# Two paired projections and a handful of ordering edges in a two-layer hybrid decoder trunk

## The chip, the core and the metric

The kernel runs on one core of a Trainium2 chip. The core has a matrix engine (TensorE, PE in the profile), a vector engine (VectorE, DVE), a scalar engine (ScalarE, ACT), a general engine (GpSimd, POOL) and a queue engine that issues transfers (SyncE, SP). The metric is the device time of one execution in microseconds (us); the median of several runs is compared.

## The reference

Two layers work on x of 256 rows and 1024 columns, in float32. Every layer normalizes the rows, multiplies by one input matrix of 1024 x 3584, runs three kinds of heads on the result, gates each with a SiLU path, multiplies by an output matrix and adds the input back:

```python
hn = rms_norm(x, norm_gain)
proj = jnp.einsum('bsd,de->bse', hn, w_in)
a_q, a_k, a_v, a_g, b_x, b_g, c_q, c_k, c_v, c_g = jnp.split(proj, _in_split_points(), axis=-1)
...
y_a = dilated_attention(qa, ka, va) * jax.nn.silu(a_g)       # 8 heads, rotary q and k
y_b = rg_lru_branch(b_x, ...) * jax.nn.silu(b_g)             # convolution and linear recurrence
y_c = stick_breaking_attention(qc, kc, vc) * jax.nn.silu(c_g)  # 4 heads
return x + jnp.einsum('bse,ed->bsd', jnp.concatenate([y_a, y_b, y_c], -1), w_out)
```

A final normalization follows the second layer. The dilated heads take softmax over three strided windows; the stick-breaking heads take products of sigmoids along the keys.

## The kernel before

**Products with a rest.** Each float32 operand is held as two parts: a rounded part (hi) and the rest that rounding left (lo). A product is hi*hi + hi*lo + lo*hi. For activations the parts are `xh` and `xl`, which lie side by side in one tile `xx`; for weights they are the tiles `whi` and `wlo`. `load_chunk` (lines 101 to 118) fetches a weight chunk of 128 x 2048 in two transfers on the SP queue, into staging tiles `st` of which there are five. ACT then rounds four pieces of 512 (line 115, `rounds`), and DVE subtracts to get the four rests (line 117, `rests`). The chunks are numbered: 3 and 4 are the stick-breaking q and k (CQ, CK), 5 and 6 the first dilated q and k (four heads each), 7 the input of the recurrence (BX), 8 and 9 the second dilated q and k, 10 to 13 the gates (CG, BG, AG), 14 to 17 the output matrix (O). `ask` requests a chunk two ahead of the one in use.

**Two forms of a projection.** `proj_b` makes the 256 outputs of a chunk as two blocks of 128, with the 256 rows of x as the moving columns. A chunk that isn't in `PAIRED[l]` takes the plain form: one PSUM bank for both blocks, and for each block 3 x 8 products of 256 columns (`mm3`, line 225), hi*xh, hi*xl and lo*xh in turn. A paired chunk takes, for each block, a bank of its own, 8 products of 512 columns, which are hi times xh and xl at once (line 344), and 8 of 256 columns, lo*xh (line 341). The bank then holds the main sum in one half and hi*xl in the other, so ACT copies that half out (`low`, line 347) and DVE adds the two (line 349). There are three banks of this kind (pool `pp`), used in turn.

**The dilated q and k.** `rotated` (line 507) calls `proj_b`, and then DVE applies the rotary table: a shuffle, two products with the table, a sum, and in layer 0 a product with the row scales `rb` (lines 519 to 524). In the plain form these read the PSUM bank; in the paired form they read the sums, of which the first lies in a scratch tile of a pool of seven. Between the two blocks of the first q stand the stick-breaking scores (`sb_scores`): 16 products (line 474), eight sigmoids on ACT, and for each of four heads two scans and a product on DVE (lines 485 and 487). Between the two blocks of the second q stand the scores of the first four dilated heads (line 548).

**The order.** The order of PE's instructions is the order of the program. On the other engines a planner orders the instructions, by its own estimate of when each can start and by program order among those that can. `dep(a, b)` adds an ordering edge: a stands behind b on their engine, with no wait of its own. The kernel has many such edges already. An engine takes its instructions strictly in that order.

**The border of the layers.** At the end of layer 0 the output products of row tile 0 (halves 0 and 1) and then of row tile 1 finish. DVE adds each to the residual `xres` (line 796). `normed` takes the squares on ACT (line 207), the scale through Ln and Exp (line 84) and multiplies on DVE (line 265); `turn` transposes the rows on PE (line 273) and splits them into the two parts (lines 217 and 218). Row tile 0 is normalized during the last output products, and row tile 1 (`xn1`) during layer 1's first products with AV (chunks 0 and 1). ACT and DVE prepare layer 1's weight chunks meanwhile.

Of the kernel before, what the change touches and what calls it, by code (L numbers as in the profile page):

```python
# [12 lines left out]
AF = mybir.ActivationFunctionType  # L13
ALU = mybir.AluOpType
# [28 lines left out]

CH_AV, CH_CV, CH_CQ, CH_CK, CH_BX, CH_CG, CH_BG, CH_AG, CH_O = 0, 2, 3, 4, 7, 10, 11, 12, 14
CH_AQ, CH_AK = (5, 8), (6, 9)
PAIRED = ((CH_BX, CH_AQ[1], CH_AK[1], CH_CG, CH_AG, CH_AG + 1), (CH_CQ, CH_CK, CH_AQ[0], CH_AK[0], CH_BX, CH_AQ[1], CH_AK[1], CH_CG, CH_BG, CH_AG, CH_AG + 1))


@with_exitstack
def trunk_kernel(ctx: ExitStack, tc: tile.TileContext, x, first_x, first, wpack, prm_d, gatew, gains, consts, rope, out):  # L50
    nc = tc.nc
    act, dve, pe, gps = nc.scalar, nc.vector, nc.tensor, nc.gpsimd
# [10 lines left out]
    def bank(pool, tag):  # L63
        return pool.tile([P, 512], F32, name=tag, tag=tag)

    def scr(w):
        return wk.tile([P, 512], F32, name="scr", tag="scr", bufs=SCR)[:, 0:w]
# [3 lines left out]
    def dep(inst, on):  # L71
        tc.add_manual_dep(inst.ins, on.ins.name, nosync)
        return inst
# [9 lines left out]
    def tab(*a, **k):  # L83
        i = dep(act.activation(*a, **k), loaded["load"])  # L84
        loaded["users"].append(i)
        return i
# [7 lines left out]
    def x_tile():  # L94
        xx = sb.tile([P, NK, 2, S], F32R, name="xx", tag="xx")
        return xx, xx[:, :, 0, :], xx[:, :, 1, :]
# [3 lines left out]
    split, rounds, rests = {}, {}, {}  # L100
# [29 lines left out]
    def weights(l, c, ahead=AHEAD):  # L130
        ask(l, c, ahead)
        return ready.pop((l, c))
# [16 lines left out]
    for k in range(NK):  # L149
# [10 lines left out]
        w = st[:, S:1024]  # L160
# [27 lines left out]
    xres = cst.tile([P, NT, D], F32, name="xres")  # L188
# [12 lines left out]
    ones = cst.tile([P, P], F32R, name="ones")  # L201
    dve.memset(ones.bitcast(F32), 1.0)

    def rms_stats(t, eng):
        sq = wk.tile([P, 2], F32, name="sq", tag="sq", bufs=2)
        for i in range(2):
            act.activation(scr(512), xres[:, t, i * 512:(i + 1) * 512], AF.Square, accum_out=sq[:, i:i + 1])
        ss = wk.tile([P, 1], F32, name="ss", tag="ss", bufs=2)
        eng.tensor_scalar(ss, sq[:, 0:1], 1.0 / D, EPS, ALU.mult, ALU.add)
        ln = wk.tile([P, 1], F32, name="lnv", tag="lnv", bufs=2)  # L210
        tab(ln, sq[:, 1:2], AF.Ln, bias=ss, scale=1.0 / D)
        rstd = wk.tile([P, 1], F32, name="rstd", tag="rstd", bufs=4)
        tab(rstd, ln, AF.Exp, scale=-0.5)
        return rstd
# [5 lines left out]
    def mm3(ps, lhs, rhs, ks, first, last, skip=False):  # L220
# [3 lines left out]
        for i, (a, b, k) in enumerate(seq):  # L224
            pe.matmul(ps, a(k), b(k), start=first and i == 0, stop=last and i == len(seq) - 1,  # L225
                      skip_group_check=skip)

    last = {}

    def finish(t, n2, ps=None, c0=0, c1=512):  # L230
        if n2 == 0:
# [27 lines left out]
    def normed(t):  # L259
        rstd = rms_stats(t, gps)  # L260
        xns = []
        for half in range(2):
            xn = scr(512)
            cs = slice(half * 512, half * 512 + 512)
            dve.scalar_tensor_tensor(xn, xres[:, t, cs], rstd, gn[:, cs], ALU.mult, ALU.mult)
            xns.append(xn)
        return xns

# [40 lines left out]
    gn = cst.tile([P, D], F32, name="gn", tag="gn")  # L309

    for l in range(L):
# [14 lines left out]
        def proj_b(c, mid=None, to=None, sc=1.0):  # L326
            pair = c in PAIRED[l]
            hi, lo = [a.rearrange("p (k c) -> p k c", c=256) for a in weights(l, c, AHEAD - 1 if mid else AHEAD)]
# [31 lines left out]
        def proj_to(dst, c, mid=None, sc=1.0):  # L360
            if c in PAIRED[l]:
                proj_b(c, mid, [dst[:, b, :] for b in range(2)], sc)
                if l == 0:
                    dve.tensor_mul(dst, dst, rb.rearrange("p (o t) -> p o t", o=1).broadcast_to([P, 2, S]))
            else:
                scaled(dst, proj_b(c, mid), sc)
# [45 lines left out]
        def scaled(dst, ps, sc=1.0):  # L412
            if l == 0:
                a, b = rows(ps)
                last["scaled"] = dve.scalar_tensor_tensor(dst, a, sc, b, ALU.mult, ALU.mult)
            else:
                act.activation(dst, v2(ps), AF.Copy, scale=sc)
# [31 lines left out]
        def head(h):  # L449
            return slice((h % 2) * HD, (h % 2) * HD + HD), h // 2, slice(h * HD, (h + 1) * HD)  # L450
# [13 lines left out]
        zs, sw = {}, {}  # L464
        halves = ((0, slice(0, 128)), (1, slice(128, 384)))

        def sb_scores():
            for p in (0, 2):
                for h in (p, p + 1):
                    zs[h] = bank(at, "s")  # L470
                for t, cs in halves:
                    for h in (p, p + 1):
                        hr, hb, _ = head(h)
                        pe.matmul(zs[h][:, cs], qc[hr, hb, t * P:(t + 1) * P], kc[hr, hb, 0:(t + 1) * P],  # L474
                                  start=t == 0, stop=True, skip_group_check=True)
            table(SIGM, [split[l, CH_AK[0]]])
            for h in range(NHC):
                z = zs[h][:, 0:384]
                bt, om = scr(384), scr(384)
                tab(om, z, AF.Sigmoid, scale=-1.0)  # L480
                tab(bt, z, AF.Sigmoid)
                w = sw[h] = wk.tile([P, 384], F32, name="sw", tag="sw", bufs=4)
                gps.memset(w[:, 127::256], 0.0)
                for lo, n in ((0, 127), (128, 255)):
                    dve.tensor_tensor_scan(w[:, lo:lo + n][:, ::-1], om[:, lo + 1:lo + 1 + n][:, ::-1],  # L485
                                           diag[:, 255 - n:255][:, ::-1], 0.0, ALU.mult, ALU.add)
                dve.tensor_mul(w, bt, w)

        def turned(tiles, h0, gs, to):
            for g in gs:  # L490
# [17 lines left out]
        def rotated(c, tiles, h0, tag, mid=None):  # L508
            dst = tiles[h0] = sb.tile([P, 2, S], F32, name=tag, tag=tag)
            tab_ = rp0 if l == 0 else rp  # L510
            pair = c in PAIRED[l]
            if pair:
                src, high = scr(S), dst[:, 1, :]
                proj_b(c, mid, [src, high])
            else:
                ps = proj_b(c, mid)
                src, high = ps[:, 0:S], ps[:, S:2 * S]
            sh = scr(S)
            dve.stream_shuffle(sh, src, SHUF)
            dve.tensor_mul(dst[:, 0, :], src, tab_[:, 0, :])  # L520
            dve.tensor_mul(sh, sh, tab_[:, 1, :])
            dve.tensor_add(dst[:, 0, :], dst[:, 0, :], sh)
            if l == 0:
                dve.tensor_mul(dst[:, 1, :], high, rb)
# [111 lines left out]

        if l > 0:
            proj_to(qc, CH_CQ, None, 0.125)
        else:
            cq_ps = proj_b(CH_CQ)  # L640
            tables()
# [6 lines left out]
        if l == 0:  # L648
            for i in range(2):
                dve.tensor_mul(rp0[:, i, :], rp[:, i, :], rb)  # L650
        rotated(CH_AQ[0], qT, 0, "q0", sb_scores)
        rotated(CH_AK[0], kT, 0, "k0")
        split_qk(0, ("yl0", "yh0"))
        sw_t, sw_heads = turned_tile()
# [9 lines left out]

        rotated(CH_AQ[1], qT, 4, "q1", second)
        if l == 0:
            for r in rests[l, CH_CG]:
                dep(r, last["min"])
            for r in last["exps"][4:]:
                dep(r, last["low"])  # L670
            for r in (*last["recs"][2:], *rests[l, CH_CG][1:]):
                dep(r, last["sum"])
# [33 lines left out]
        ps = None  # L706
        if CH_AG in PAIRED[l]:
            agf = sb.tile([P, 2, S], F32, name="agf", tag="cg")
# [10 lines left out]
        if l == 0:  # L719
# [16 lines left out]
            for r in (*rests[l, CH_O][4:], *rests[l, CH_O + 1]):  # L736
                dep(r, last["sum", CH_AG, 0])
        if CH_AG + 1 in PAIRED[l]:
            seeded = last["bank"]
# [8 lines left out]
        o_ps = {}  # L748
# [4 lines left out]
        for n2 in range(2):  # L753
            w = weights(l, CH_O + n2)
# [23 lines left out]
        for t in range(NT):  # L778
            if t == 1 and l == 0:
                next_x = x_tile()  # L780
                xn0 = normed(0)
            for n2 in range(2):
                cs = slice(n2 * 512, n2 * 512 + 512)
                if tail and (t, n2) == (1, 1):
                    for ps, c0, c1 in tail:
                        out_mm(ps, ow[n2], t, 1, range(4), False, True, c0, c1, c0 > 0)
                        if c0 == 0:
                            x_t = xres[:, t, 512:512 + LATE]
                            dve.tensor_add(x_t, ps, x_t)
                        finish(t, n2, None if c0 == 0 else ps, c0, c1)  # L790
                    continue
                for ks in ((0, 1), (2, 3)):
                    out_mm(o_ps[t, n2], ow[n2], t, 1, ks, False, ks[0] == 2)
                    if (l, t, n2, ks[0]) == (0, 1, 1, 0):
                        turn(xn0, 0, *next_x[1:])
                dve.tensor_add(xres[:, t, cs], o_ps[t, n2], xres[:, t, cs])
                if l > 0:
                    finish(t, n2)

# [106 lines left out]
```

## Time and profile before

| what | value |
|---|---|
| median of 3 runs | 245.24 us (244.14 to 245.63) |
| the profiled execution | 245.22 us |
| its span, first to last instruction | 243.3 us |
| PE busy | 235.7 us, 97% of the span |
| PE's weight loads busy | 203.3 us, 84% |
| DVE busy | 202.3 us, 83% |
| ACT busy | 176.8 us, 73% |
| granted TensorE clock | 0.995 of full |
| transfers | 43.88 MB, mean 180 GB/s |

The shares are averages over the span. What an engine's busy time is worth depends on whether something waits for it, so the chain of waits and the order of the queues around a stage count for more than the shares. An instruction's start and length are given in microseconds from the start of the span; weight loads (PEld) run beside products (PE). The recorded lengths of neighbours on DVE and ACT overlap a little; the distance from start to start is what an instruction occupies of its queue.

### The profile page before, as it was taken

The numbers are of one execution on the slowest core, as the hardware profiler recorded it, in microseconds if no ns is written. First come the engines' busy times: TensorE is split into PE (matmuls) and PEld (weight loads), VectorE is DVE, ScalarE is ACT, GpSimd is POOL, SyncE is SP. The second block draws the span as 40 slices with busy tenths as digits, with TensorE's granted clock in tenths as the row PEclk, the third lists the DMA queues.
The fourth block names the chain that finished last, engine by engine and source line by source line (L and its number), as shares of the span: only waits on it lengthen the run. The fifth ranks groups of instructions, "written<-read, shape, count | busy, mean of one in ns | idle before, by whom it ended". The sixth has DMA issues, their size and how long they took to land.

```text
span 243.3 us, 4455 instructions
## 1 busy us (share of the span) xinstructions
PE 235.7 (97%) x1587; PEld 203.3 (84%) x1587; DVE 202.3 (83%) x488; ACT 176.8 (73%) x392; POOL 11.5 (5%) x43
## 2 busy tenths in 40 slices
PE   8799999999999999999999999999999999999991
PEld 4688999988888888878888888888988888887881
DVE  3695798999999979998795675999999986997362
ACT  3678985929947889986773775876669858997243
POOL 0017200001000000000010000000010000000000
PEclk9999999999999999999999999999999999999998
DMA  6999998565266832278747387606570772000022
GB/s 187 387 290 389 392 283 259 174 207 172 51 220 209 267 123 88 64 231 294 275 145 276 103 288 252 204 32 185 164 216 13 244 267 72 14 0 3 0 86 88
DMA packets 14037, 43.88 MB, mean 180 GB/s; under 512 B 1728, under 2 KB 3008, under 8 KB 14016
## 3 DMA queue, kind: packets, MB, share of 16 engines
q1 hardware_dynamic: 13248, 42.43, 52.2%
q0 software_dynamic: 192, 0.52, 0.8%
q10 hardware_dynamic: 576, 0.66, 0.8%
q8 instruction: 12, 0.20, 0.3%
q14 instruction: 9, 0.07, 0.1%
HBM read 42.03 MB, written 1.05 MB: 177 GB/s over the span
## 4 chain that ended last, share of the span: by engine, by line
PE 94%; DMA 2%; DVE 1%; SPq 0%; ACT 0%; issue 0%; DVEq 0%
PE pp L344 26%; PE pp L225 25%; PE pp L341 14%; PE s L225 9%; PE s L181 4%; PE s L494 3%; DMA st<-first 2%; PE y L458 2%; PE pp L385 2%; PE s L548 2%; PE pp L181 2%; PE s L474 1%; PE y L225 1%; PE pp L458 1%; PE s L609 1%; PE s L273 1%
## 5 line engine op out<-in xcount | busy, mean ns | idle before, releaser
L117 DVE TENSOR_TENSOR wlo<-st,whi 128x512 fp32r<-128x512 f32 x128 | 82.2, 683 | 6.8 <-ACT whi L115 6.1
L115 ACT ACTIVATE whi<-st 128x512 fp32r<-128x512 f32 x130 | 73.5, 630 | 12.7 <-DMA st<-w_pack 9.2
L344 PE MATMUL pp<-xx,whi 128*128 128x512 f32 x272 | 66.5, 393 | 0.0
L344 PEld LDWEIGHTS pp<-xx,whi 128*128 128x128 f32 x272 | 49.4, 188 | 9.7 <-DVE q L349 0.3
L341 PEld LDWEIGHTS pp<-xx,wlo 128*128 128x128 f32 x272 | 35.2, 191 | 2.1 <-ACT scr L84 0.3
L341 PE MATMUL pp<-xx,wlo 128*128 128x256 f32 x272 | 36.8, 285 | 0.0
L225 PE MATMUL pp<-xx,whi 128*128 128x256 f32 x160 | 21.1, 285 | 0.0
L225 PEld LDWEIGHTS pp<-xx,whi 128*128 128x128 f32 x160 | 19.8, 191 | 0.5 <-issue 0.3
L347 ACT ACTIVATE low<-pp 128x256 f32<-128x256 f32 x34 | 12.5, 373 | 10.4 <-PE pp L344 9.6
L78 ACT ACT_TABLE_LOAD x13 | 16.7, 1283 | 1.9 <-PEq L899 1.7
L84 ACT ACTIVATE pr<-scr,mn 128x128 f32<-128x128 f32 (+1 forms) x32 | 14.1, 443 | 3.9 <-DVE mn L555 3.9
L225 PE MATMUL pp<-whi,yh 128*128 128x512 f32 (+1 forms) x48 | 14.1, 382 | 0.0
L225 PE MATMUL pp<-wlo,yh 128*128 128x512 f32 (+1 forms) x48 | 13.7, 372 | 0.0
L225 PE MATMUL pp<-whi,yl 128*128 128x512 f32 (+1 forms) x48 | 13.6, 371 | 0.0
L225 PE MATMUL pp<-xx,wlo 128*128 128x256 f32 x80 | 11.2, 283 | 0.0
L181 PE MATMUL s<-whi,xx 128*128 128x512 f32 (+1 forms) x36 | 9.8, 394 | 1.2 <-ACT xx L161 1.2
L225 PEld LDWEIGHTS pp<-xx,wlo 128*128 128x128 f32 x80 | 10.3, 192 | 0.0
L225 PEld LDWEIGHTS pp<-whi,yl 128*128 128x128 f32 x48 | 8.6, 188 | 1.6
L225 PEld LDWEIGHTS pp<-wlo,yh 128*128 128x128 f32 x48 | 8.6, 188 | 1.6
L225 PEld LDWEIGHTS pp<-whi,yh 128*128 128x128 f32 x48 | 8.3, 188 | 1.6 <-issue 0.3
L555 DVE CUSTOM_DVE_ANT_0 scr<-s,con 128x128 f32<-128x128 f32 (+1 forms) x32 | 9.2, 352 | 0.0
L485 DVE TENSOR_TENSOR_SCAN sw<-scr,con 128x127 f32<-128x127 f32 (+1 forms) x16 | 7.9, 537 | 1.1 <-ACT scr L84 1.1
(193 smaller groups left out, 374.9 us busy)
## 6 DMA issues: line engine op xcount, KB each, us to landing
st<-w_pack SPq DMA_DIRECT2D x66, 512.0 KB, 5.1
st<-first SPq DMA_DIRECT2D x7, 512.0 KB, 6.8
xres<-x_in SPq DMA_DIRECT2D x4, 256.0 KB, 6.7
gw_t<-gate_w SPq DMA_DIRECT2D x2, 256.0 KB, 6.9
gn<-gains SPq DMA_DIRECT2D x2, 256.0 KB, 6.5
xs<-xc POOLq DMA_DIRECT2D x4, 128.0 KB, 3.2
gf<-gains SPq DMA_DIRECT2D x2, 256.0 KB, 5.0
out<-st ACTq DMA_DIRECT2D x2, 192.0 KB, 2.0
```

The costliest lines, as they stand in the source:

```text
L78: load = act.preload_act_table_set(name)
L84: i = dep(act.activation(*a, **k), loaded["load"])
L115: split[l, c] = act.activation(h, part, AF.Copy)
L117: rests.setdefault((l, c), []).append(dve.tensor_sub(r, part, h.bitcast(F32)))
L181: pe.matmul(ps[t][:, c0:c1], a[:, k, t * P:(t + 1) * P], b, start=k == 0 and all(m[0] is not ps for m in seq[:i]), stop=k == NK - 1 and al ...
L225: pe.matmul(ps, a(k), b(k), start=first and i == 0, stop=last and i == len(seq) - 1, skip_group_check=skip)
L341: pe.matmul(ps[:, 0:S], lo[:, k, cs], xh[:, k, :], start=i == 0, stop=i == len(seq) - 1, skip_group_check=True)
L344: pe.matmul(ps, hi[:, k, cs], xx[:, k].rearrange("p h t -> p (h t)"), start=i == 0, stop=i == len(seq) - 1, skip_group_check=True)
L347: last["low"] = last["low", c, b] = act.activation(low, ps[:, S:2 * S], AF.Copy, scale=sc)
L458: pe.matmul(y[hr, p * 128 + o:p * 128 + 256], vt[:, s0, hs], wts[i][s0], start=s0 == 0, stop=s0 == 1)
L485: dve.tensor_tensor_scan(w[:, lo:lo + n][:, ::-1], om[:, lo + 1:lo + 1 + n][:, ::-1], diag[:, 255 - n:255][:, ::-1], 0.0, ALU.mult, ALU.add)
L555: last["min"] = dve.tensor_tensor_reduce(xs[:, cs], sps[h][:, cs], nmask[:, cs], -0.125, 3e38, ALU.add, ALU.min, mn[:, t:t + 1])
```

## The change

Chunks 5 and 6 of layer 0 (the first dilated q and k) join the paired chunks of that layer, so both take the 512-wide form that layer 1 already uses for them. Ordering edges are added in five places; nothing else changes in what is computed. In the order of the program: the DVE products of stick-breaking heads 2 and 3 stand behind the sum of q's first block; the four rests of chunk 8 stand behind the sum of k's first block; at the border, rests 1 to 3 of layer 1's chunk 1 stand behind the first residual addition of row tile 0 and rests 2 and 3 behind its second one; roundings 2 and 3 of that chunk stand behind the first square; in layer 1, rests 1 to 3 of CQ stand behind row tile 1's normalization.

```diff
-PAIRED = ((CH_BX, CH_AQ[1], CH_AK[1], CH_CG, CH_AG, CH_AG + 1), (...))
+PAIRED = ((CH_BX, CH_AQ[0], CH_AK[0], CH_AQ[1], CH_AK[1], CH_CG, CH_AG, CH_AG + 1), (...))
...
         for i in range(2):
-            act.activation(scr(512), xres[:, t, i * 512:(i + 1) * 512], AF.Square, accum_out=sq[:, i:i + 1])
+            last["square", i] = act.activation(scr(512), xres[:, t, i * 512:(i + 1) * 512], AF.Square,
+                                               accum_out=sq[:, i:i + 1])
...
-            dve.scalar_tensor_tensor(xn, xres[:, t, cs], rstd, gn[:, cs], ALU.mult, ALU.mult)
+            last["norm"] = dve.scalar_tensor_tensor(xn, xres[:, t, cs], rstd, gn[:, cs], ALU.mult, ALU.mult)
...
-                dve.tensor_mul(w, bt, w)
+                last["sw", h] = dve.tensor_mul(w, bt, w)
...
         if l > 0:
             proj_to(qc, CH_CQ, None, 0.125)
+            for r in rests[l, CH_CQ][1:]:
+                dep(r, last["norm"])
...
         rotated(CH_AQ[0], qT, 0, "q0", sb_scores)
+        if l == 0:
+            for h in (2, 3):
+                dep(last["sw", h], last["sum", CH_AQ[0], 0])
         rotated(CH_AK[0], kT, 0, "k0")
...
         rotated(CH_AQ[1], qT, 4, "q1", second)
         if l == 0:
+            for r in rests[l, CH_AQ[1]]:
+                dep(r, last["sum", CH_AK[0], 0])
...
                 next_x = x_tile()
+                for i in range(2):
+                    for r in rests[1, CH_AV + 1][1 + i:]:
+                        dep(r, last["add", i])
                 xn0 = normed(0)
+                for r in rounds[1, CH_AV + 1][2:]:
+                    dep(r, last["square", 0])
...
-                dve.tensor_add(xres[:, t, cs], o_ps[t, n2], xres[:, t, cs])
+                last["add", n2] = dve.tensor_add(xres[:, t, cs], o_ps[t, n2], xres[:, t, cs])
```

More of the change, by code (lines that the diff above doesn't have):

```diff
@@ L45 @@
 CH_AQ, CH_AK = (5, 8), (6, 9)
-PAIRED = ((CH_BX, CH_AQ[1], CH_AK[1], CH_CG, CH_AG, CH_AG + 1), (CH_CQ, CH_CK, CH_AQ[0], CH_AK[0], CH_BX, CH_AQ[1], CH_AK[1], CH_CG, CH_BG, CH_AG, CH_AG + 1))
+PAIRED = ((CH_BX, CH_AQ[0], CH_AK[0], CH_AQ[1], CH_AK[1], CH_CG, CH_AG, CH_AG + 1), (CH_CQ, CH_CK, CH_AQ[0], CH_AK[0], CH_BX, CH_AQ[1], CH_AK[1], CH_CG, CH_BG, CH_AG, CH_AG + 1))
 @with_exitstack
@@ L202, in trunk_kernel @@
     dve.memset(ones.bitcast(F32), 1.0)
+    last = {}
     def rms_stats(t, eng):
@@ L226, in mm3 @@
                       skip_group_check=skip)
-    last = {}
     def finish(t, n2, ps=None, c0=0, c1=512):
```

## The prediction

> **What bounds the kernel now.** I read the chain of waits in order of time first. Times are microseconds from the start of the span, then the length, then the work.
>
> ```profile
> span 243.3 us, 4455 instructions
> ...
> 32.31 5.75 PE pp L225 x48
> 38.06 1.51 PE s L474 x16
> 39.57 8.83 PE pp L225 x72
> 48.41 1.84 PE pp L344 x8
> ...
> 51.20 0.44 PE s L494 x4
> ...
> 120.58 0.88 PE s L273 x8
> ...
> 122.83 5.44 PE s L225 x24
> 128.28 0.96 PE s L273 x8
> ...
> 149.57 3.65 PE pp L344 x16
> 153.22 0.95 PE pp L341 x8
> 154.17 1.51 PE s L474 x16
> 155.69 1.15 PE pp L341 x8
> ...
> 160.49 1.91 PE pp L341 x16
> 162.41 3.65 PE pp L344 x16
> ```
>
> Each piece starts where the one before ended, and all are TensorE (PE). The end is therefore set by how long PE's products take, and any other engine counts only where it makes PE wait. The profiled execution took 245.22 us, 1.92 more than its span; I make the sum against 245.22, which lies 0.02 under the median of 245.24.
>
> The changed stage runs from the first block of the first dilated q (chunk 5) to the start of chunk BX. Half of the 48 products at 32.31 are still CK's, so it starts at 32.31 + 2.87 = 35.18 and ends at 48.41. Layer 1 runs the same steps already in the form that the change gives to layer 0. There the stage starts half way through the piece at 149.57, which is 151.39, and ends half way through the one at 162.41, which is 164.23. The view of busy time by stretch puts the two side by side (stretch, length, then busy time and instructions of PE, PE's weight loads, DVE and ACT; PEclk is the granted clock):
>
> ```profile
> 35.18:48.41 13.23, 13.23 (x114) 12.72 (x113) 12.13 (x27) 10.59 (x21) 0.00 (x0) 1.00 0.70 232
> 151.39:164.23 12.84, 12.84 (x82) 11.04 (x81) 12.10 (x28) 10.46 (x22) 0.00 (x0) 1.00 0.37 126
> ```
>
> PE is busy for the whole of both. DVE has 1.1 us to spare in layer 0, so its queue must be followed next.
>
> **The products.** The old form has 48 products of 256 columns in a chunk: 5.75 us. The new form has 16 of 512 and 16 of 256: 3.65 + 1.91 = 5.56 us. That is 0.19 less, and 0.38 for the two chunks; the two stretches give 13.23 - 12.84 = 0.39 with all that lies between. I take 0.38. Both forms stream 6,144 columns through PE, so what is saved is the time that each of the 16 dropped products costs beside its columns. By the rows a 256-wide one takes 5.75/48 = 0.120 us and a 512-wide one 3.65/16 = 0.228, so a product costs about 0.012 beside its columns, and 16 times 0.012 is 0.19.
>
> The Trainium skill, in "TensorE: Matmul & The Clock Gate", section "Back-to-back issue gap", puts a warm isolated product at its columns over 2.4 GHz plus 2.5 ns, and itself says that pairs of weight load and product run at another pace. By its formula a chunk would go from 5.24 to 5.20 us, and the gain of both would be 0.08 instead of 0.38. The trace does not agree with that size: 0.120 us and 0.228 us stand where the formula gives 0.109 and 0.216.
>
> **What the new form adds.** Each block now ends with one ACT copy (low) and one DVE sum, four of each for the two chunks. The shuffle and the four products and sums of the rotation stay, now reading the summed tile. From the page's groups, and the views in order of time of DVE and ACT (start, length, line, tiles, shapes, count; brackets: idle time before it and what ended that):
>
> ```profile
> L347 ACT ACTIVATE low<-pp 128x256 f32<-128x256 f32 x34 | 12.5, 373 | 10.4 <-PE pp L344 9.6
> ```
>
> ```profile
> 38.95 3.17 ACT L84 ACTIVATE scr<-s 128x384 f32<-128x384 f32 x8 [2.50 <-PE s L474]
> ...
> 58.75 2.19 ACT L115 ACTIVATE whi<-st 128x512 fp32r<-128x512 f32 x4
> ```
>
> ```profile
> 39.47 1.31 DVE L485 TENSOR_TENSOR_SCAN sw<-scr,con 128x127 f32<-128x127 f32 x3 [1.10 <-ACT scr L84]
> ...
> 46.14 0.45 DVE L519 STREAM_SHUFFLE scr<-pp 128x256 f32<-128x256 f32 x1
> ...
> 47.81 2.49 DVE L117 TENSOR_TENSOR wlo<-st,whi 128x512 fp32r<-128x512 f32 x4
> ...
> 154.80 0.42 DVE L349 TENSOR_TENSOR scr<-pp,low 128x256 f32<-128x256 f32 x1
> 155.25 0.42 DVE L520 TENSOR_TENSOR q<-scr,rp 128x256 f32<-128x256 f32 x1
> 155.60 0.99 DVE L485 TENSOR_TENSOR_SCAN sw<-scr,con 128x127 f32<-128x127 f32 x2
> ...
> 164.78 0.41 DVE L349 TENSOR_TENSOR scr<-pp,low 128x256 f32<-128x256 f32 x1
> ```
>
> ACT: 4 x 0.37 = 1.5 us at most. The first low falls into the 2.50 us in which ACT waits for the stick-breaking scores; the others push its weight roundings, which have room (below). I cost ACT at nothing.
>
> DVE: the five rotation steps from 46.14 to 47.81 take 1.67 us, so an operation of this shape occupies the queue for 0.334 and four sums for 1.34. In layer 1 the first sum and one product of the rotation stand ahead of the scans. Layer 0 has an idle 1.10 us at that place, so these two would fill 0.67 of it, and DVE runs 1.34 - 0.67 = 0.67 us later than before from there on. The bounds are 0.34, if the shuffle fits as well, and 1.34, if nothing does.
>
> PSUM: three banks go round, so a block needs the bank of the third block before it. PE starts the second block of the first k at about 45.06, BX's blocks at 47.85 and, with 0.44 of transposes between, 51.08. The first needs the sum of q's first block, which the new edge puts ahead of the third and fourth heads' stick-breaking products, so it comes out between the scans that begin at 39.47 at the latest. The second needs the sum of q's second block: where the shuffle stood, at 46.14 plus up to 0.67, so about 1 us is spare. The third needs the sum of k's first block. Behind the four residuals of chunk 8 (at 47.81) it would come at about 50.9 and end after 51.08; the new edge puts the residuals behind it, and it ends near 49, with 2 us spare. So that edge pays for what the pairing would cost. Those residuals then end about 1 us later than 50.30. They also hold back the staging buffers that SP's next weight transfers wait for:
>
> ```profile
> st<-w_pack SPq DMA_DIRECT2D x66, 512.0 KB, 5.1
> ```
>
> 51.3 + 5.1 is 56.4, and ACT rounds the chunk that arrives there (11) at 58.75: 2.3 us spare. PE uses chunk 8's residuals only after BX's second block (51.08 + 2.79 = 53.9) and eight wide products (1.84), at 55.7: 4 us spare. So SP and PE lose nothing.
>
> **Where the delay on DVE comes out.** DVE has no idle time above 0.1 us from 39.47 until 88.67. The delay of 0.67 reaches the gate of the recurrence (BG) and its chain:
>
> ```profile
> 86.19 0.68 DVE L415 SCALAR_TENSOR_TENSOR scr<-pp,rb 128x512 f32<-128x512 f32 x1
> ...
> 90.06 0.42 DVE L349 TENSOR_TENSOR agf<-pp,low 128x256 f32<-128x256 f32 x1 [1.39 <-ACT low L347]
> ...
> 97.53 0.68 DVE L447 TENSOR_TENSOR yl<-scr,yh 128x512 fp32r<-128x512 f32 x1
> ```
>
> ```profile
> 86.90 0.64 ACT L84 ACTIVATE scr<-scr 128x512 f32<-128x512 f32 x1 [0.70 <-DVE scr L415]
> ...
> 96.72 0.63 ACT L446 ACTIVATE yh<-scr 128x512 fp32r<-128x512 f32 x1 [0.34 <-DVE scr L444]
> ```
>
> ```profile
> 98.11 0.41 PEld L225 LDWEIGHTS s<-whi,yh 128*128 128x128 f32 x2
> ...
> 99.01 0.41 PEld L225 LDWEIGHTS s<-whi,yl 128*128 128x128 f32 x2
> ```
>
> The 1.39 us of idle DVE at 90.06 is no cushion: ACT was late because its sigmoid at 86.90 waited for DVE's 86.19. At the other end the rounded half yh is done at 97.35 and PE loads it at 98.11, a margin of 0.76; the rest yl is done at 98.21 and loaded at 99.01, a margin of 0.80. With PE 0.38 earlier the margin is 0.38, so a delay of 0.67 makes PE wait 0.29. Bounds: nothing at 0.34, 0.96 at 1.34. I take 0.29, because layer 1's order is the nearest row.
>
> **The border between the layers.** The edges put the first tile's two residual additions ahead of three of the residuals of chunk (1, 1), two roundings of that chunk behind a square, and three residuals of CQ behind the second tile's normalization.
>
> ```profile
> 116.41 0.68 DVE L796 TENSOR_TENSOR xres<-s,xres 128x512 f32<-128x512 f32 x1
> ...
> 119.12 1.42 DVE L265 SCALAR_TENSOR_TENSOR scr<-xres,rstd,gn 128x512 f32<-128x512 f32 x2 [1.43 <-ACT rstd L84]
> ...
> 125.25 1.89 DVE L117 TENSOR_TENSOR wlo<-st,whi 128x512 fp32r<-128x512 f32 x3
> 127.05 1.41 DVE L265 SCALAR_TENSOR_TENSOR scr<-xres,rstd,gn 128x512 f32<-128x512 f32 x2
> ```
>
> ```profile
> 126.23 0.20 ACT L84 ACTIVATE rstd<-lnv 128x1 f32<-128x1 f32 x1
> ```
>
> The first tile's normalized rows are ready at 120.54 and their transposes start at 120.58, the second half half-way through them: 0.48 of margin, which the earlier additions widen. The second tile's rows end at 128.46, during the transposes that begin at 128.28; these take 0.96 where the same eight took 0.88, so 0.08 is waited there. The scale is known at 126.43, so without the residuals ahead the rows end 0.6 earlier. I take -0.08; bounds 0 and -0.12. The moved residuals of (1, 1) are needed some 3.6 us into the piece at 122.83, near 126.4; they end by 119. The transfers behind them move by at most 2 us and feed layer 1's CQ at 140 and later. Those of CQ end near 130 and are also used past 140.
>
> **Sum.** -0.38 + 0.29 - 0.08 = -0.17: 245.22 - 0.17 = 245.05. What lies past the border follows PE unchanged.
>
> **Rivals.** (a) The order on DVE absorbs less, so that the delay is 0.85 to 1.34: PE's wait is 0.47 to 0.96 and the time 245.2 to 245.7. For it: the queue is full for 49 us. Against it: layer 1's order. (b) PE is bound by columns, and 6,144 stay 6,144: no gain in products, no wait at 98, only the border, 245.14. The two stretches speak against it. This is where the skill's formula, with its 0.08, would nearly lead. (c) The edges don't act, with chunk 8's residuals still ahead of the sum: BX's second block waits 0.25, the border's 0.08 stays, 245.4. Against it: an edge fixes the order on one engine. (d) Slower: each sum stands at the head of DVE's queue until its low is done, as at 90.06 for 1.39 us. Four such waits and the 0.67 make a delay of 6.2, PE waits 5.85 at 98, and the time is 250.6. It passes +1% once the waits add up to some 2.6 us, 0.66 for each sum. Against it: in layer 1 the rows of 154.80 and 164.78 have no bracket, so those sums did not wait.
>
> **How the numbers follow.** Forecast 0.66 (244.76 to 245.2), (a) 0.18, (b) 0.03, (c) 0.05, (d) 0.05, and 0.03 for a gain of over 1%, for which I see no mechanism: 2.4 us would have to come out of a PE that does not wait. About 1% is what a measurement of this kernel can tell from no change; the three runs went from 244.14 to 245.63. The range goes from 244.76 to 245.72 by the bounds, and reaches 0.8 below and 0.4 above for that scatter: 243.9 to 246.1. Faster 0.03, within 1% 0.92, slower 0.05.
>
> **What would show it.** Right: the stage of layer 0 at 12.8 us; four sums of 0.41 at L349 (new numbering aside) without brackets, the first ahead of the scans; the loads of yh near 98 waiting for ACT by a few tenths; the second transposes at 0.88. Wrong: the stage still at 13.2 (b), a weight load in BX that waits for a sum (c), or idle DVE in front of the sums and a PE wait of microseconds before 100 (d). If PE does not wait at 98 the gain is 0.46.

## The result, and the profile after

The changed kernel takes 246.56 us at the median, and its ratio to the kernel before is 1.0053, with a 95% interval of 1.0034 to 1.0072: some 1.3 us slower, where 0.17 us faster was forecast and the range ended at 246.1. One of its seven runs took 475.36 us, and the ratio is taken without it. By the bound of the prediction the change is still "within 1%", but the loss is real, the sign was wrong, and 246.56 lies above the range.

The page of the changed kernel, its first and third row and the shares of the chain of waits:

```profile
span 244.6 us, 4394 instructions
...
PE 237.4 (97%) x1555; PEld 202.6 (83%) x1555; DVE 203.6 (83%) x492; ACT 178.4 (73%) x396; POOL 10.5 (4%) x43
...
PE 81%; DVE 14%; DMA 2%; issue 1%; ACT 0%; SPq 0%; DVEq 0%
```

The busy times of PE, DVE and ACT have moved by less than 1%. What is new is that the chain leaves PE for DVE over 14% of the span. The changed stage itself did what was forecast. First the view of busy time by stretch of the changed kernel (stretch, length, PE, weight loads, DVE, ACT), then its chain in order of time, where half of the old piece at 32.31 now stands alone in front of the stage:

```profile
35.66:48.50 12.84, 12.84 (x82) 11.01 (x81) 12.14 (x27) 10.89 (x22) 0.00 (x0) 1.00 0.68 225
```

```profile
32.78 2.88 PE pp L228 x24
35.66 1.84 PE pp L345 x8
...
49.65 2.41 DVE wlo L117 x4
...
71.06 1.22 PE pp L342 x8
72.28 1.84 PE pp L345 x8
...
129.88 0.88 PE s L274 x8
```

The stage takes 12.84 us instead of 13.23, and the second transposes of the border 0.88 instead of 0.96. The stage starts at 35.66 and not at 35.18, although PE's program up to there is the same; in the thirteen profiles of this study that start lies between 33.9 and 35.7. So profiles are compared below by the stage's clock, the time since PE began the first block of the first dilated q. From the stage's start to the last instruction the kernel before takes 243.3 - 35.18 = 208.1 us and the changed one 244.6 - 35.66 = 208.9: a loss of 0.8 us, although PE had won 0.39 by the stage's end. So 1.2 us went behind the stage.

**Where PE waits.** PE's weight loads of the changed kernel, three of their waits behind the stage (in brackets the idle time before, and what ended it):

```profile
71.06 1.01 PEld L342 LDWEIGHTS pp<-xx,wlo 128*128 128x128 f32 x8 [0.40 <-DVE scr L350]
...
78.64 0.14 PEld L610 LDWEIGHTS s<-xs,gw_t 64*64 64x64 f32 x2 [0.20 <-ACT pa L496]
...
113.72 0.30 PEld L228 LDWEIGHTS s<-whi,yh 128*128 128x128 f32 x2 [0.38 <-ACT yh L447]
```

At 71.06 the second block of chunk CG waits for a PSUM bank, that is, for the DVE sum of the third block before it, the first of chunk 9. At 78.64 the gates of the recurrence stand behind copies on ACT. At 113.72 a rounded y is late. One more wait for ACT, of 0.22 us, lies at 105; a pause of 0.35 us at 108 stands in the kernel before as well. The place that the prediction named, the loads of yh at 98, shows no wait.

**Why DVE is late.** DVE's view in order of time, before and after (the stage's clock is 35.18 and 35.66 less):

```profile
50.23 0.44 DVE L519 STREAM_SHUFFLE scr<-pp 128x256 f32<-128x256 f32 x1
...
60.56 0.28 DVE L555 CUSTOM_DVE_ANT_0 scr<-s,con 128x128 f32<-128x128 f32 x1
...
68.61 0.41 DVE L349 TENSOR_TENSOR scr<-pp,low 128x256 f32<-128x256 f32 x1
```

```profile
36.95 1.28 DVE L117 TENSOR_TENSOR wlo<-st,whi 128x512 fp32r<-128x512 f32 x2
38.91 0.42 DVE L350 TENSOR_TENSOR scr<-pp,low 128x256 f32<-128x256 f32 x1 [0.67 <-ACT low L348]
39.36 0.43 DVE L521 TENSOR_TENSOR q<-scr,rp 128x256 f32<-128x256 f32 x1
39.71 0.69 DVE L117 TENSOR_TENSOR wlo<-st,whi 128x512 fp32r<-128x512 f32 x1
40.31 1.31 DVE L486 TENSOR_TENSOR_SCAN sw<-scr,con 128x127 f32<-128x127 f32 x3
...
45.31 0.66 DVE L117 TENSOR_TENSOR wlo<-st,whi 128x512 fp32r<-128x512 f32 x1
...
47.91 0.44 DVE L520 STREAM_SHUFFLE scr<-scr 128x256 f32<-128x256 f32 x1
...
52.32 0.45 DVE L520 STREAM_SHUFFLE scr<-scr 128x256 f32<-128x256 f32 x1
...
62.54 0.28 DVE L556 CUSTOM_DVE_ANT_0 scr<-s,con 128x128 f32<-128x128 f32 x1
...
70.59 0.42 DVE L350 TENSOR_TENSOR scr<-pp,low 128x256 f32<-128x256 f32 x1
```

At the shuffle of k, DVE stands at 50.23 - 35.18 = 15.05 before and at 52.32 - 35.66 = 16.66 after: 1.61 us late, where the prediction had 0.67 and a bound of 1.34. At the dilated scores (60.56 and 62.54) it is 1.50 late, and at the sum for which PE waits (68.61 and 70.59) again 1.50. The first sum and a product of the rotation do stand ahead of the scans, as forecast. But DVE idles 0.67 us in front of that sum, and of the four rests of chunk 7 only one comes before the scans, where two did so in the kernel before. ACT's view shows why, before and after:

```profile
33.62 1.28 ACT L78 ACT_TABLE_LOAD   x1
35.30 1.15 ACT L115 ACTIVATE whi<-st 128x512 fp32r<-128x512 f32 x2 [0.40 <-DMA st<-w_pack]
```

```profile
35.31 1.28 ACT L78 ACT_TABLE_LOAD   x1
38.49 0.38 ACT L348 ACTIVATE low<-pp 128x256 f32<-128x256 f32 x1 [1.90 <-PE pp L342]
38.77 0.62 ACT L115 ACTIVATE whi<-st 128x512 fp32r<-128x512 f32 x1
39.34 2.79 ACT L84 ACTIVATE scr<-s 128x384 f32<-128x384 f32 x7
...
42.55 1.66 ACT L115 ACTIVATE whi<-st 128x512 fp32r<-128x512 f32 x3
```

Before, ACT made the first two roundings of chunk 7 (35.30) and then waited 2.50 us for the scores. After, the new copy low stands ahead of those roundings and waits 1.90 us for PE at the head of ACT's queue. One rounding follows it, the other three come behind the sigmoids. So the two rests that filled DVE before 38.4 can't be made yet, DVE idles, and the work comes back later. This is how the 1.61 us add up: the scans start 0.36 late (40.31 - 35.66 against 39.47 - 35.18), one rest of 0.60 has moved behind them, three further sums cost 0.33 each, and the product that is done early gives 0.33 back: 0.36 + 0.60 + 1.00 - 0.33 = 1.63, against the 1.61 of the two rows. The forecast had the last two terms alone.

The Trainium skill, "TensorE: Matmul & The Clock Gate", section "Architectural detail: the array is 16× 32×32, not 1× 128×128", states that the queues of ScalarE and VectorE are strictly first in, first out. The rows of 38.49 and 38.77 agree: the rounding follows the copy without a gap, after 1.90 us in which ACT began nothing.

### The profile page after: what moved, and what is told of

Read it like the earlier page. It is cut to its first block, busy times and chain, and to the rows that moved or that the text cites. A ratio compares the mean times of both kernels' runs of the same rounds, so it can differ in the third digit from the quotient of the medians.

```text
span 244.6 us, 4394 instructions
## 1 busy us (share of the span) xinstructions
PE 237.4 (97%) x1555; PEld 202.6 (83%) x1555; DVE 203.6 (83%) x492; ACT 178.4 (73%) x396; POOL 10.5 (4%) x43
## 4 chain that ended last, share of the span: by engine, by line
PE 81%; DVE 14%; DMA 2%; issue 1%; ACT 0%; SPq 0%; DVEq 0%
PE pp L345 21%; PE pp L228 20%; PE pp L342 11%; PE s L228 9%; PE s L181 4%; DVE wlo L117 4%; PE s L495 3%; DMA st<-first 2%; PE y L459 2%; PE pp L386 2%; PE pp L181 2%; PE s L549 2%; DVE sw L486 1%; PE y L228 1%; PE pp L459 1%; PE s L610 1%
## 5 line engine op out<-in xcount | busy, mean ns | idle before, releaser
L345 PE MATMUL pp<-xx,whi 128*128 128x512 f32 x304 | 74.1, 393 | 0.0
L345 PEld LDWEIGHTS pp<-xx,whi 128*128 128x128 f32 x304 | 55.3, 188 | 10.9 <-DVE q L350 0.3
L342 PEld LDWEIGHTS pp<-xx,wlo 128*128 128x128 f32 x304 | 39.4, 191 | 3.0 <-DVE scr L350 0.4
L342 PE MATMUL pp<-xx,wlo 128*128 128x256 f32 x304 | 41.5, 285 | 0.2 <-DVE scr L350 0.2
L348 ACT ACTIVATE low<-pp 128x256 f32<-128x256 f32 x38 | 14.0, 374 | 10.6 <-PE pp L345 8.0
L228 PE MATMUL pp<-xx,whi 128*128 128x256 f32 x96 | 13.2, 287 | 0.0
L228 PEld LDWEIGHTS pp<-xx,whi 128*128 128x128 f32 x96 | 12.0, 191 | 0.6 <-ACT whi L115 0.4
L181 PE MATMUL s<-whi,xx 128*128 128x512 f32 (+1 forms) x36 | 10.4, 409 | 0.8 <-ACT xx L161 0.7
L181 PEld LDWEIGHTS s<-whi,xx 128*128 128x128 f32 x36 | 6.6, 216 | 2.4 <-ACT xx L161 1.4
L571 DVE TENSOR_SCALAR pr<-pr,den 128x128 f32<-128x128 f32 (+1 forms) x32 | 8.5, 313 | 0.1
L228 PE MATMUL s<-whi,xx 128*128 128x512 f32 x32 | 8.3, 390 | 0.0
```

Source lines behind the costliest of these rows:

```text
L181: pe.matmul(ps[t][:, c0:c1], a[:, k, t * P:(t + 1) * P], b, start=k == 0 and all(m[0] is not ps for m in seq[:i]), stop=k == NK - 1 and al ...
L342: pe.matmul(ps[:, 0:S], lo[:, k, cs], xh[:, k, :], start=i == 0, stop=i == len(seq) - 1, skip_group_check=True)
L345: pe.matmul(ps, hi[:, k, cs], xx[:, k].rearrange("p h t -> p (h t)"), start=i == 0, stop=i == len(seq) - 1, skip_group_check=True)
L348: last["low"] = last["low", c, b] = act.activation(low, ps[:, S:2 * S], AF.Copy, scale=sc)
L571: dve.tensor_scalar(pr[:, cs], pr[:, cs], den[:, t:t + 1], None, ALU.mult)
```

## The experiments

The table has each kernel's profile by the stage's clock: how late DVE is at the first reduction of the dilated scores (25.38 us after the stage's start in the kernel before), and how much later the last instruction comes (208.12 before). Each is one profiled execution, with its span read to 0.1 us; the ratios come from repeated runs beside the kernel before.

| kernel | DVE late at the scores, us | end later, us | ratio, 95% interval |
|---|---|---|---|
| the changed kernel | 1.50 | 0.82 | 1.0053 (1.0034 to 1.0072) |
| e1 pair alone | 1.50 | 1.22 | 1.0067 (1.0045 to 1.0089) |
| e2 border alone | 0.00 | -0.09 | 1.0004 (0.9987 to 1.0022) |
| e3 four DVE products left out | 1.10 | 0.41 | 1.0026 (1.0009 to 1.0044) |
| e4 before, four DVE sums more | 1.20 | 1.06 | 1.0048 (1.0025 to 1.0071) |
| e5 q alone paired | 0.95 | 0.72 | 1.0026 (1.0005 to 1.0048) |
| e6 products on POOL | 1.82 | 1.61 | 1.0050 (1.0030 to 1.0069) |
| e7 copies first | 1.49 | 0.65 | 1.0041 (1.0019 to 1.0063) |
| e8 POOL and copies | 1.82 | 1.14 | 1.0049 (1.0030 to 1.0068) |
| e9 roundings first | 0.37 | 0.48 | 1.0014 (0.9992 to 1.0035) |
| e10 roundings and copies | 0.57 | -0.21 | 1.0013 (0.9993 to 1.0032) |
| e11 q alone, roundings first | -0.18 | -0.01 | 1.0000 (0.9979 to 1.0021) |

**e1, the pair alone.** The kernel before with only the line of paired chunks changed, no new edges.

```diff
-PAIRED = ((CH_BX, CH_AQ[1], CH_AK[1], CH_CG, CH_AG, CH_AG + 1), (...))
+PAIRED = ((CH_BX, CH_AQ[0], CH_AK[0], CH_AQ[1], CH_AK[1], CH_CG, CH_AG, CH_AG + 1), (...))
```

> The kernel before with the two chunks paired and none of the ordering edges. Theory (the four added sums lengthen VectorE's full queue, and what waits behind it makes TensorE wait): about the whole loss stays, 246.3 to 247.0 us, with the 0.1 us of the border on top of the changed kernel. Rival (the ordering edges are what costs): 244.8 to 245.0 us, the products' 0.38 us gained. Rival (the loss is chance in the first 30 us, ahead of the change): 244.8 to 245.2 us.

It is slower by 0.67%, which is 246.9 us beside the 245.24 before, as the theory had it. DVE is as late as in the changed kernel, so the edges don't cause that. PE now also waits in BX; its weight loads, and DVE's order, in this kernel:

```profile
51.82 1.01 PEld L341 LDWEIGHTS pp<-xx,wlo 128*128 128x128 f32 x8 [0.63 <-DVE scr L349]
```

```profile
49.54 1.89 DVE L117 TENSOR_TENSOR wlo<-st,whi 128x512 fp32r<-128x512 f32 x3
51.35 0.41 DVE L349 TENSOR_TENSOR scr<-pp,low 128x256 f32<-128x256 f32 x1
```

This is the wait of the prediction's rival (c): with three of chunk 8's four rests ahead of the sum of k's first block, BX's second block waits for its bank. It came to 0.63 us instead of the 0.25 given there, in a kernel whose DVE was later than assumed. In the changed kernel the edge takes this wait away. In these two profiles that is worth 1.22 - 0.82 = 0.4 us; the intervals of the two ratios overlap.

**e2, the border alone.** The kernel before with the three groups of edges at the border.

```diff
+                for i in range(2):
+                    for r in rests[1, CH_AV + 1][1 + i:]:
+                        dep(r, last["add", i])
                 xn0 = normed(0)
+                for r in rounds[1, CH_AV + 1][2:]:
+                    dep(r, last["square", 0])
...
+            for r in rests[l, CH_CQ][1:]:
+                dep(r, last["norm"])
```

> The kernel before with the edges at the layers' border alone, nothing paired. Theory: 245.1 us, 0.1 us below before, and TensorE's second transposes take 0.88 us in place of 0.96. Rival (the edges cost): 246 us or more, with TensorE waiting between 110 and 140 us.

No difference that can be measured. The second transposes take 0.88 us here too, and the profile's 0.09 us is near the size forecast, but no larger than what the rounding of the two spans can make.

**e3, less work on DVE.** The changed kernel without the products of the unrotated halves with the row scales: four in layer 0, two of them in the changed chunks. The queries and keys of the dilated heads are thus left unscaled in those halves.

```diff
-            if l == 0:
-                dve.tensor_mul(dst[:, 1, :], high, rb)
```

> The changed kernel without the four products of the unrotated half of q and k with the row scales in layer 0 (left out of the computation): VectorE has 4 x 0.334 = 1.34 us less to do between 45 and 76 us, as much as the four added sums brought. Theory: TensorE's waits at 71, 78, 82 and 113 us mostly go, and the time falls to 244.8 to 245.4 us. Rival (something else than VectorE's queue: the order, the banks, the start): 246.2 to 246.8 us as the changed kernel.

By the ratios about half of the loss goes (1.0026, or 245.9 us beside 245.24), though the two intervals overlap; that lies between the theory and the rival and in the range of neither. PE keeps its lead through the bank of CG at 71, and then waits 0.41 us at the gates for ACT's copies.

**e4, the kernel before with four sums more.** Four DVE additions of the same shape, whose results nobody reads, in the first q and k of the kernel before; the products stay in the plain form.

```diff
+            if l == 0 and not pair:
+                for i in range(2):
+                    junk = wk.tile([P, S], F32, name="low", tag="low", bufs=2)
+                    dve.tensor_add(junk, (src, high)[i], rb)
```

> The kernel before, nothing paired and no edge, with four more VectorE operations of 128x256 from PSUM (two ahead of each rotation of chunks 5 and 6 in layer 0, results unused). Theory: VectorE runs 1.34 us later from 46 us on, which nothing absorbs; TensorE waits 0.4 to 1.0 us after 70 us, 245.6 to 246.2 us. Rival (VectorE's queue has slack, the loss is the pairing's banks, copies or order): 245.2 us.

With no paired product, no added copy on ACT and no edge, 1.20 us of lateness on DVE cost 0.48%, 1.06 us by the stage's clock and a little more than the theory had. DVE's queue behind the stage is a bound that the chain before, all PE, did not show. The prediction's own margin at 98, 0.76 for a PE that is not early, would have let 0.44 of these 1.20 us through.

**e5, q alone.** The changed kernel with the first k left plain, and so without the edge for k's sum.

```diff
-PAIRED = ((CH_BX, CH_AQ[0], CH_AK[0], CH_AQ[1], CH_AK[1], CH_CG, CH_AG, CH_AG + 1), (...))
+PAIRED = ((CH_BX, CH_AQ[0], CH_AQ[1], CH_AK[1], CH_CG, CH_AG, CH_AG + 1), (...))
...
-            for r in rests[l, CH_AQ[1]]:
-                dep(r, last["sum", CH_AK[0], 0])
```

> The changed kernel with only the first dilated q in the wide form; the first k stays plain, and the edge that holds chunk 8's rests back behind k's sum falls away with it. Theory (the full DVE queue takes back what PE wins): two sums instead of four, of 0.34 us each, and the first sum and a product of the rotation lie in the idle 1.1 us before the scans, so DVE is at most 0.3 us late afterwards, PE is 0.19 earlier at the next chunk and loses 0 to 0.3 of it later: a ratio to the kernel before of 0.999 to 1.002. Rival (each paired chunk costs the same, whatever its place on DVE): half of the measured loss, a ratio of about 1.0027.

A miss: two sums, of which one was to be hidden, still make DVE 0.95 late, and the ratio is the rival's. Two sums occupy 0.67 us, so the number of sums alone can't make 0.95, and the place of the first one comes into question.

**e6, e7 and e8, two reliefs.** In e6 the four products of e3 are not left out but made on POOL. In e7 the third and fourth rounding of chunk 13 stand behind ACT's copies pa and pb. e8 has both.

```diff
-                dve.tensor_mul(dst[:, 1, :], high, rb)
+                gps.tensor_mul(dst[:, 1, :], high, rb)
```

```diff
         pts = dil_transposes(0)
+        turned_copy = last["copy"]
...
+            for r in rounds[l, CH_AG + 1][2:]:
+                dep(r, turned_copy)
```

> The changed kernel with the product of the unrotated halves and the row scales (four operations of 0.34 us on DVE's queue) on POOL, which is otherwise idle. Nothing is left out. Theory: DVE is relieved as in the run that left this product out, so the ratio to the kernel before is about that run's 1.0026, at most 0.001 more if POOL's slower product is awaited by the rounding of q and k. Rival (POOL's product comes so late that the split of q and k, and with it the dilated scores, waits): 1.005 and more, with a wait for POOL ahead of the rounding of q or k.

> The changed kernel with two more ordering edges on ACT: the third and fourth rounding of chunk 13 stand behind the three copies of the transposed dilated weights (pa, pb), instead of the third ahead of them. The copies then need not wait for chunk 13's second transfer, which is 1.4 us later than in the kernel before. Theory (that transfer, late because the rests behind it are late, holds the copies and so the gates' and values' start): the copies begin at 76.7 instead of 78.0, PE's wait at the gates and values (0.4 to 0.6 us) goes, and the ratio falls from 1.0053 to 1.002 to 1.004. Rival (DVE's own lateness meets PE again in the next step that needs it): PE is earlier after the values but the end is within 0.15 us of the changed kernel, 1.005.

> The changed kernel with both: the four products on POOL and the two edges behind the copies. If the two causes add (DVE's queue, and the transfer ahead of the copies), what is left of the loss is the first one's 0.0026 less the 0.4 us at the gates, so a ratio of 0.999 to 1.001. If they are the same loss seen twice, the ratio stays at the better one of the two alone.

e6 gained nothing: DVE is later than in the changed kernel, 1.82 at the scores. POOL's and DVE's rows of e6:

```profile
47.27 0.74 POOL L525 TENSOR_TENSOR q<-q,rb 128x256 f32<-128x256 f32 x1 [21.08 <-DVE q L350]
51.78 0.74 POOL L525 TENSOR_TENSOR k<-k,rb 128x256 f32<-128x256 f32 x1 [3.77 <-DVE k L350]
```

```profile
47.59 0.71 DVE L522 TENSOR_TENSOR scr<-scr,rp 128x256 f32<-128x256 f32 x1
...
51.97 0.83 DVE L521 TENSOR_TENSOR k<-scr,rp 128x256 f32<-128x256 f32 x1
```

DVE's product beside POOL's takes 0.71 and 0.83 us instead of 0.42, and it ends 0.29 and 0.28 us after POOL's does (48.30 against 48.01, 52.80 against 52.52). That fits a DVE that stood still until POOL was done. So each product moved to POOL freed 0.33 us of DVE's queue and cost its neighbour there 0.29 or 0.41; where the rest of the 1.82 comes from was not followed.

e7 shows how one wait gives place to the next. ACT's copies, before and after, stand behind a rounding that waits for a transfer:

```profile
76.06 0.63 ACT L115 ACTIVATE whi<-st 128x512 fp32r<-128x512 f32 x1 [1.23 <-DMA st<-w_pack]
76.60 1.07 ACT L495 ACTIVATE pa<-s 128x512 f32<-128x512 f32 x2
```

```profile
77.47 0.63 ACT L115 ACTIVATE whi<-st 128x512 fp32r<-128x512 f32 x1 [0.77 <-DMA st<-w_pack]
78.01 1.06 ACT L496 ACTIVATE pa<-s 128x512 f32<-128x512 f32 x2
```

By the stage's clock that transfer is 0.93 late. In e7 the copies are made at 75.56 and PE waits neither at the gates nor at the values; at the scores that follow, it waits instead:

```profile
75.56 1.08 ACT L496 ACTIVATE pa<-s 128x512 f32<-128x512 f32 x2
```

```profile
81.63 0.41 PEld L549 LDWEIGHTS s<-k,q 32*128 32x128 f32 x9 [0.34 <-ACT it L84]
```

The end came 0.17 us earlier than in the changed kernel, less than half of the 0.4 to 0.6 that the theory wanted, and the ratio, 1.0041, is not apart from the changed kernel's. e8 (1.0049) is no better than e6; its sum of two reliefs could not come, since e6 relieved nothing.

**e9, e10 and e11, the order on ACT.** The changed kernel with low of q's first block behind the first two roundings of chunk 7 (e9). e10 adds the edges of e7, e11 has them on e5.

```diff
         if l == 0:
+            for i in range(2):
+                dep(last["low", CH_AQ[0], 0], rounds[l, CH_BX][i])
             for h in (2, 3):
                 dep(last["sw", h], last["sum", CH_AQ[0], 0])
```

> The changed kernel with two more ordering edges on ACT: the copy low of q's first block stands behind the first two roundings of chunk 7 (BX). In the changed kernel that copy stands ahead of them and waits 1.90 us for PE at the head of ACT's queue; DVE finds neither the sum nor those two rests and idles 0.67 us, and the rests come after the scans instead of before them. Theory (this order, more than the four sums themselves, makes DVE 1.6 us late at the rotation of k): the two rests are done before the first sum, DVE is 0.1 to 0.6 us late at that rotation, PE keeps most of its 0.39 through the block of CG that waited at 71, and the ratio to the kernel before falls from 1.0053 to 0.9985 to 1.0015. Rival (the four sums have to be paid wherever the queue is full, 1.34 us): 1.003 to 1.005.

> The changed kernel with the edges of the roundings first and, besides, those that put the third and fourth rounding of chunk 13 behind the copies of the transposed weights. If DVE's lateness is what holds the rests, the staging buffers and the transfers back, the second pair of edges has little left to gain: within 0.1 us of the run with the roundings first alone. If the transfer ahead of the copies is late by itself, 0.2 to 0.4 us faster than that run, a ratio of 0.997 to 1.000.

> Only the first dilated q in the wide form, with the roundings of chunk 7 ahead of its first copy low. Theory: DVE is 0.9 us late in the run with q alone and 0.96 us earlier by the order (0.36 at the scans and one rest of 0.60), so it is not late at all, PE keeps its 0.19 and the border's 0.08: a ratio of 0.9985 to 1.000. Rival (the wide form has a price that no order removes): 1.002 and more, as without the edges.

In e9 ACT and then DVE read:

```profile
35.69 1.16 ACT L115 ACTIVATE whi<-st 128x512 fp32r<-128x512 f32 x2 [0.60 <-DMA st<-w_pack]
37.63 0.38 ACT L348 ACTIVATE low<-pp 128x256 f32<-128x256 f32 x1 [0.78 <-PE pp L342]
```

```profile
35.57 2.48 DVE L117 TENSOR_TENSOR wlo<-st,whi 128x512 fp32r<-128x512 f32 x4
38.05 0.42 DVE L350 TENSOR_TENSOR scr<-pp,low 128x256 f32<-128x256 f32 x1
38.56 0.69 DVE L117 TENSOR_TENSOR wlo<-st,whi 128x512 fp32r<-128x512 f32 x1
39.17 1.31 DVE L486 TENSOR_TENSOR_SCAN sw<-scr,con 128x127 f32<-128x127 f32 x3
...
50.32 0.44 DVE L520 STREAM_SHUFFLE scr<-scr 128x256 f32<-128x256 f32 x1
```

The sum has no bracket any more, three rests of chunk 7 lie before the scans, and with the stage's start at 34.80 the shuffle of k comes at 15.52, 0.47 late instead of 1.61. The sums are the same four, and so is the work of every engine. Two edges are new, and with them the planner's order in the stage: a third rest comes ahead of the scans, and the first product of the rotation behind them. The 0.47 adds up too: scans 0.08 late, three further sums, and one rest more than before ahead of the scans, 0.08 + 1.00 - 0.60. So e9 does not only take the wait away, it also fills DVE's idle time better than the kernel before did. The ratio falls from 1.0053 to 1.0014, in the theory's range, though the upper end of its interval reaches the rival's. That the place of one ACT copy made DVE late is shown; how much of the loss it made is known only roughly: 0.0039 of 0.0053 by the ratios, whose intervals just touch, and 0.34 of 0.82 us by the two profiles. PE keeps its 0.39 until the gates, where it now waits longer than in the changed kernel, since it comes earlier and the transfer does not. The kernel before, and then e9:

```profile
77.72 0.14 PEld L609 LDWEIGHTS s<-xs,gw_t 64*64 64x64 f32 x2
```

```profile
77.68 0.14 PEld L610 LDWEIGHTS s<-xs,gw_t 64*64 64x64 f32 x2 [0.55 <-ACT pa L496]
```

By the stage's clock PE loads these weights at 42.54 before and at 42.88 in e9: it comes to the gates 0.39 early and leaves them 0.34 late. In e10 this wait is gone, and its profile ends 0.21 us earlier than that of the kernel before. The runs don't bear out the difference to e9 (1.0013 against 1.0014), so what the second pair of edges is worth stays open. e11 is level with the kernel before, to 0.2% either way; against e5, from which it differs by the two edges alone, DVE goes from 0.95 late to 0.18 early and the ratio from 1.0026 to 1.0000, in intervals that overlap. No version here is measurably faster than the kernel before: the whole gain of the products is 0.39 us, 0.16% of the time.

## Why the prediction was wrong

**Right.** The products: 0.39 us for the stage (0.38 forecast). The border: 0.88 us, and nothing measurable from e2. The PSUM banks in BX: no wait there with the edge, and the wait of rival (c) without it (e1). DVE as the resource on which the change would be paid for, with no idle time behind the scans. Two slips changed nothing: 6,144 columns are one block's, and a chunk streams 12,288 in both forms; and by the stage's length of 12.84, BX starts at 48.02 and not at 47.85.

**The step that failed first** is the cost of ACT: "The first low falls into the 2.50 us in which ACT waits for the stick-breaking scores ... I cost ACT at nothing." That idle time came after two roundings. The step asked whether ACT had time, not what would stand behind the copy while it waited. The copy was put ahead of the roundings, held them back while it waited 1.90 us, and held back with them the rests that DVE needed to fill its own time. e9 undoes this, and DVE's lateness at k falls from 1.61 to 0.47.

**The term that followed from it**, the 0.67 us of delay on DVE, was therefore 1.61. Its upper bound, 1.34, was no bound: it held the added sums, and not work that the new order moves from before the scans to behind them (0.36 + 0.60). I took layer 1's order as the nearest row, but looked at its DVE queue alone and not at what its ACT queue had ahead of the copy. There, in the kernel before, four roundings stand ahead of the copy of q's first block, which then waits only 0.30 us:

```profile
151.73 2.18 ACT L115 ACTIVATE whi<-st 128x512 fp32r<-128x512 f32 x4
154.21 0.38 ACT L347 ACTIVATE low<-pp 128x256 f32<-128x256 f32 x1 [0.30 <-PE pp L341]
```

**The outlet** was the second step that failed, and it failed by itself. Between BX and the border only the loads at 98 were given a margin, and "SP and PE lose nothing" followed no transfer later than chunk 11's. The first place was the bank of CG's second block at 71. In the kernel before, the sum ends at 68.61 + 0.41 = 69.02, and PE comes to that block half way through this piece of the chain, at 70.79:

```profile
69.83 1.91 PE pp L341 x16
```

That is a margin of 1.77; PE earlier by 0.39 and DVE later by 1.50 use it up. The wide products behind that block begin at 69.83 + 1.91 - 35.18 = 36.56 before and at 72.28 - 35.66 = 36.62 after, so PE loses 0.45 there and is 0.06 late instead of 0.39 early. At the gates, which wait for the transfer of chunk 13, it is 0.44 late (42.54 before, 78.64 - 35.66 = 42.98 after), and further waits follow at the scores and at y. In e7 the wait at the gates goes and the one at the scores takes its place, and the end moved little. e10 does not fit that picture: without the wait at the gates its profile keeps PE early to the end, and only the runs show no gain over e9.

e9's profile shows what the outlet alone is worth. Its DVE is 0.47 late at k and 0.37 at the scores, and 0.67 late (28.41 against 27.74 by the stage's clock) at the first rest of chunk 10, before and in e9:

```profile
62.92 0.67 DVE L117 TENSOR_TENSOR wlo<-st,whi 128x512 fp32r<-128x512 f32 x1
```

```profile
63.21 0.67 DVE L117 TENSOR_TENSOR wlo<-st,whi 128x512 fp32r<-128x512 f32 x1
```

So up to there DVE is no later than the 0.67 of the prediction, which was to cost PE 0.29. But PE loses 0.73 at the gates alone, and the profile ends 0.48 late instead of 0.17 early. The order on ACT set how late DVE was; that the outlets lay earlier, and had less room, is why even the forecast delay would have cost more than the products gain, as far as one profile can show it.

**The rivals.** (a), a longer delay on DVE, was the nearest, but its times ended at 245.7 by the same bound. With 1.61 its own formula, delay less the margin of 0.38, gives 1.23 us of waiting and 245.22 - 0.46 + 1.23 = 246.0, near the end measured by the stage's clock (208.94 against 208.12). That is luck: the formula has the wait at 98, where there was none. (d), a sum at the head of DVE's queue, happened once, for 0.67 us, and its cause was the same thing one queue earlier. The chance of 0.92 for "within 1%" was right; within it, the sign was not.

## What to carry to other kernels

An added instruction that waits costs what stands behind it in its own queue, on every engine that it passes through; ask this of the copy as well as of the sum, and give the new wait an edge that lets ready work go first. Idle time that ends in a wait says nothing about the work just ahead of it, and where an engine has run full for tens of microseconds a delay is bounded only if every piece of work that the new order moves is in the bound. List all the places where the critical engine needs the late one, with their margins: removing the wait that shows can leave the next one to take its place.

## What was not expected of the hardware

A DVE product with both inputs in SBUF took 0.71 and 0.83 us beside a POOL product, where it takes 0.42 alone, and ended some 0.28 us after POOL's (e6). The Trainium skill, "SBUF — State Buffer", section "Who interferes with whom", states that such a DVE instruction contends with a GpSimd instruction that reads SBUF, that the port pair which the two share is an exclusive lock, and that the order of issue decides who blocks; the rows of 47.59 and 51.97, both issued after POOL's, agree. Apart from that, the start of the changed stage lay anywhere between 33.9 and 35.7 us in thirteen profiles with the same PE program up to there, a spread of 1.8 us, which is more than the whole loss under study. Its cause was not looked into, and a comparison of two single profiles by their spans would have been misled by it.
